# Attention's operands in the mixer's own tiles, and a product split around the first scores

## The chip, the cores and the metric

One core of a Trainium2 chip runs the whole program: TensorE (PE, with its weight loads shown apart as PEld), VectorE (DVE), ScalarE (ACT), GpSimd (POOL) and SyncE (SP), the last of which only issues transfers. The metric is the device time of one execution in microseconds; of several runs the median is taken. There is one input shape (512 tokens, width 1024, two layers), all in float32.

## The reference

Each of the two layers adds three sub-layers to a residual stream: half a SwiGLU block, a mixer, and another half SwiGLU block. The change lies in the mixer, which runs three token mixers on one normalised input:

```python
h = rms_norm(x, mix_norm[l]) @ w_mix_in[l]
(c_x, c_b, c_c, h_q, h_f, h_i, h_g, f_q, f_k, f_v, f_f) = jnp.split(h, split_at, axis=-1)
y = concat[short_conv_mixer(c_x, c_b, c_c, conv_w[l]),           # 256 channels, width 3
           hgrn2_mixer(h_q, h_f, h_i, h_g, lower_bounds[l], ...),  # 4 heads of 64, a gated recurrence
           fox_mixer(f_q, f_k, f_v, f_f, ...)]                   # 8 heads of 64, causal softmax attention
x = x + y @ w_mix_out[l]
# fox_mixer: q, k normalised per head; logit[t, s] = q_t . k_s + c_t - c_s,  c = cumsum(log f);  o = softmax(logit) @ v
```

## The kernel before

**How numbers are carried.** A float32 product is made of three TensorE products: each operand is split into a rounded high part and the rest (`hi`, `lo`), and `mm3` issues hi·hi, hi·lo and lo·hi (lines 376, 382, 383 of the profile). Weights come by SP into a ring of two tiles `st`; ACT writes the high part and DVE the low part into a ring of three tiles `hl` (lines 362 and 363). Accumulators are PSUM banks in four rings: three `mm`, two `sc`, two `pt`, one `po`.

**The order of work.** The program is traced in Python, and a scheduler then orders each engine's instructions at compile time by priority and readiness. `follow(engine, i)` pins an instruction behind the last one that was given so on that engine. Each engine then runs its instructions strictly in that order. A tile of a pool's ring (a "tag") can be written again once its last reader has finished, and a pool that is opened after another was closed lies on the same addresses, so its tiles wait for the last readers of the old tiles there.

**The mixer.** `mix` opens a pool `mp` for the whole mixer. Inside it a pool `hp` ("hg") holds HGRN2: gates and the tiles `q, S, kb, b` (pairs, one per pair of heads; `b` is the running sum of the log gates, `kb` the key's exponent against it, `S` the recurrent state). HGRN2's two pairs of heads run as generators of 13 steps; beside steps 3 to 22 one step each is drawn from `dense`, which makes attention's normalised queries and keys `qk` (two halves of four heads) and the values `V`. These are token-major products: four banks `mm, mm, mm, po` of 128 tokens, the activation stationary on TensorE, the weight moving. For `V` there are 8 steps of 12 products; 20 of dense's 24 steps fit beside HGRN2, so 4 steps of `V` (48 products) are left when HGRN2 is done.

Then `hp` is closed, and a pool `ap_` ("at") is opened on its addresses. `fox_attend` yields step by step, and between its steps `BESIDE` says how many steps of `rest()` are drawn: the rest of `dense`, then the short convolution's products (`conv`), then most of the output projection.

**Attention's operands.** For each head, `fox_prep` transposes queries and keys into a `pt` bank (line 1526), ACT and DVE write the high and the low part (lines 1530 and 1531) to two tiles of the ring `t`, and SP copies them in six transfers of 64 partitions (line 1538) into four stacked operands, `QA, KA` (128 rows) and `QB, KB` (66 rows, with the decay `negc` in the last two; line 1522). Heads alternate between two sets of these tiles. `scores` multiplies them in `sc` banks (line 1565), `turn` transposes the softmax weights (line 1602), `values` multiplies them with `V` (line 1620). The heads' scores come in two parts: part 0 for the first 256 queries, part 1 for the others.

All of `QA, KA, QB, KB`, and the two tiles of ring `t` between, lie in `ap_`, that is, on `hp`'s addresses. HGRN2's last instruction in `hp` is the read of line 1424, which makes the low part `hy` of its output.

## Time and profile before

| | us |
|---|---|
| median of 3 runs | 1849.82 |
| lowest and highest | 1848.95, 1850.83 |
| the profiled execution | 1855.04 |
| its span | 1853.0 |
| mean granted TensorE clock | 0.993 |
| first scores, layer 0 and layer 1 (start of line 1565) | 486.95, 1400.15 |

The profiled execution is 5.2 us (0.28%) longer than the median of the runs, and its span is 2.0 us shorter than its own time. All places below are microseconds from the start of the span. Rows of a timeline give start, duration, engine, line, operation, destination and sources, the shape, and in brackets how long the engine had been idle and what released it. A row of the view by windows gives, for each engine, busy time with the number of instructions, then the granted clock, the share of time that the 16 DMA engines were busy, and GB/s.

### The profile page before, as it was taken

The numbers are of one execution on the slowest core, as the hardware profiler recorded it, in microseconds if no ns is written. First come the engines' busy times: TensorE is split into PE (matmuls) and PEld (weight loads), VectorE is DVE, ScalarE is ACT, GpSimd is POOL, SyncE is SP. The second block draws the span as 40 slices with busy tenths as digits, with TensorE's granted clock in tenths as the row PEclk, the third lists the DMA queues.
The fourth block names the chain that finished last, engine by engine and source line by source line (L and its number), as shares of the span: only waits on it lengthen the run. The fifth ranks groups of instructions, "written<-read, shape, count | busy, mean of one in ns | idle before, by whom it ended". The sixth has DMA issues, their size and how long they took to land.

```text
span 1853.0 us, 32031 instructions
## 1 busy us (share of the span) xinstructions
PE 1831.0 (99%) x12939; PEld 1681.2 (91%) x12939; DVE 1447.7 (78%) x1965; ACT 1004.4 (54%) x1415; POOL 184.7 (10%) x190
## 2 busy tenths in 40 slices
PE   9999999999899999999999999999998999999999
PEld 6899999888788899999989999998887888999997
DVE  7889887679576888878678887966786777987883
ACT  5455554465566555555445555545655664555552
POOL 0011120100000011112001111201000001021210
PEclk9999999999899999999999999999998999999999
DMA  7658784242343667868266787823324429577662
GB/s 204 182 119 191 182 177 96 69 127 69 97 111 101 206 136 180 183 172 171 76 199 139 171 187 186 171 58 89 107 69 112 123 86 238 140 158 199 147 144 91
DMA packets 249908, 262.38 MB, mean 142 GB/s; under 512 B 19816, under 2 KB 228464, under 8 KB 249760
## 3 DMA queue, kind: packets, MB, share of 16 engines
q1 hardware_dynamic: 193344, 191.63, 34.6%
q0 software_dynamic: 55840, 68.19, 23.1%
q8 instruction: 101, 1.65, 0.4%
q10 hardware_dynamic: 576, 0.52, 0.1%
q14 instruction: 47, 0.39, 0.1%
HBM read 226.15 MB, written 2.17 MB: 123 GB/s over the span
## 4 chain that ended last, share of the span: by engine, by line
PE 94%; DVE 3%; ACT 2%; DMA 1%; issue 1%; SPq 0%; DVEq 0%; ACTq 0%
PE mm L376 14%; PE mm L383 13%; PE mm L382 13%; PE sc L376 6%; PE sc L382 6%; PE sc L383 6%; PE pt L376 6%; PE pt L382 6%; PE pt L383 6%; PE po L376 3%; PE po L383 3%; PE po L382 3%; PE sc L1565 2%; PE po L1620 1%; PE sc L1382 1%; PE pt L1602 1%
## 5 line engine op out<-in xcount | busy, mean ns | idle before, releaser
L809 ACT CAST hl<-w 128x1024 fp32r<-128x1024 f32 x322 | 337.6, 1050 | 346.7 <-PE mm L383 81.9
L811 DVE TENSOR_TENSOR hl<-w,hl 128x1024 fp32r<-128x1024 f32 x322 | 393.0, 1222 | 86.1 <-ACT hl L809 85.9
L363 DVE TENSOR_TENSOR hl<-st,hl 128x1024 fp32r<-128x1024 f32 (+3 forms) x152 | 160.2, 1054 | 128.4 <-ACT hl L362 127.9
L362 ACT CAST hl<-st 128x1024 fp32r<-128x1024 f32 (+3 forms) x152 | 138.7, 912 | 176.8 <-PE po L383 83.4
L376 PE MATMUL mm<-xc,hl 128*128 128x256 f32 (+1 forms) x730 | 201.5, 276 | 0.3 <-ACT g L908 0.3
L383 PE MATMUL mm<-xc,hl 128*128 128x256 f32 x728 | 201.4, 277 | 0.0
L382 PE MATMUL mm<-xc,hl 128*128 128x256 f32 x728 | 201.3, 277 | 0.0
L376 PE MATMUL sc<-xc,hl 128*128 128x256 f32 (+1 forms) x530 | 146.4, 277 | 0.6 <-ACT g L908 0.6
L383 PE MATMUL sc<-xc,hl 128*128 128x256 f32 x528 | 146.2, 277 | 0.0
L382 PE MATMUL sc<-xc,hl 128*128 128x256 f32 x528 | 146.1, 277 | 0.0
L376 PEld LDWEIGHTS mm<-xc,hl 128*128 128x128 f32 x730 | 137.0, 188 | 0.8 <-ACT g L908 0.5
L382 PEld LDWEIGHTS mm<-xc,hl 128*128 128x128 f32 x728 | 136.9, 188 | 0.0
L383 PEld LDWEIGHTS mm<-xc,hl 128*128 128x128 f32 x728 | 136.7, 188 | 0.1
L376 PE MATMUL pt<-xc,hl 128*128 128x256 f32 (+1 forms) x482 | 132.7, 276 | 0.0
L382 PE MATMUL pt<-xc,hl 128*128 128x256 f32 x480 | 132.7, 276 | 0.0
L383 PE MATMUL pt<-xc,hl 128*128 128x256 f32 x480 | 132.6, 276 | 0.0
L376 PE MATMUL mm<-x,hl 128*128 128x512 f32 x272 | 111.0, 408 | 0.0
L382 PE MATMUL mm<-x,hl 128*128 128x512 f32 x272 | 107.4, 395 | 0.0
L383 PE MATMUL mm<-x,hl 128*128 128x512 f32 x272 | 107.3, 394 | 0.0
L376 PEld LDWEIGHTS sc<-xc,hl 128*128 128x128 f32 x530 | 99.6, 188 | 1.5 <-ACT g L908 1.0
L383 PEld LDWEIGHTS sc<-xc,hl 128*128 128x128 f32 x528 | 99.1, 188 | 0.1
L382 PEld LDWEIGHTS sc<-xc,hl 128*128 128x128 f32 x528 | 99.2, 188 | 0.0
(478 smaller groups left out, 5489.0 us busy)
## 6 DMA issues: line engine op xcount, KB each, us to landing
w<-in_ffn_w_in_dram SPq DMA_DIRECT2D x140, 512.0 KB
w<-in_ffn_w_out_dram SPq DMA_DIRECT2D x64, 512.0 KB
w<-in_ffn_w_out_dram POOLq DMA_DIRECT2D x56, 512.0 KB, 8.4
st<-in_w_mix_in_dram SPq DMA_DIRECT2D x80, 256.0 KB
w<-in_ffn_w_in_dram POOLq DMA_DIRECT2D x39, 512.0 KB, 8.0
st<-in_ffn_w_in_dram SPq DMA_DIRECT2D x70, 256.0 KB
w<-S POOLq DMA_DIRECT2D x35, 512.0 KB, 4.7
st<-in_ffn_w_out_dram SPq DMA_DIRECT2D x24, 512.0 KB
```

What stands on the lines that cost most here:

```text
L362: a = nc.scalar.copy(hi, src[:, c : c + w])
L363: b = nc.vector.tensor_sub(lo, src[:, c : c + w], hi)
L376: i = nc.tensor.matmul(acc[:, c], ah, bh[:, c], start=first and c.start == 0, stop=False, skip_group_check=True,)
L382: nc.tensor.matmul(acc, ah, bl, start=False, stop=False, skip_group_check=True)
L383: i = nc.tensor.matmul(acc, al, bh, start=False, stop=last, skip_group_check=True)
L809: A(nc.scalar.copy(hi, src))
L811: return lambda: V(nc.vector.tensor_sub(lo, src, hi))
L1382: nc.tensor.matmul(s2[:, :, t], e[:, i * P : (i + 1) * P], e2[:, :, t], start=True, stop=True)
L1565: mm = lambda *a, **k: E(nc.tensor.matmul(*a, skip_group_check=True, **k))
L1602: E(nc.tensor.transpose(tb[:, k * P : (k + 1) * P], to[u][:, j * P : (j + 1) * P], self.ident))
L1620: E(nc.tensor.matmul(self.ob[:, o], half[2][:, j, h].rearrange("p a d -> p (a d)"), part[:, at[0] : at[-1] + 1, :].rearrange("p b t -> p ( ...
```

## The change

```diff
-BESIDE = (2, 2, 1) + (1, 1, 2, 2, 1, 2, 2) + (1, 2, 2, 2, 2, 2, 1, 2, 2)
+BESIDE = (3, 2, 1) + (1, 1, 2, 1, 1, 2, 2) + (1, 2, 2, 2, 2, 2, 1, 2, 2)
...
                 elif not (halves and acc is jobs[-1][0]):
-                    self.mm3(acc, ah[:, toks], al[:, toks], hi[:, cols], lo[:, cols], first, stop)
+                    self.mm3(
+                        acc, ah[:, toks], al[:, toks], hi[:, cols], lo[:, cols], first, stop, False, keep
+                    )
...
-                q, S, kb, b = (pair(hp, tag) for tag in ("q", "S", "kb", "b"))
+                b, kb, q, S = (pair(mp, tag) for tag in ("b", "kb", "q", "S"))
+                negc = mp.tile([NH, 2, T], F32R, tag="n", name=self.n("negc"))
...
             with tc.tile_pool(name=self.n("at"), bufs=1) as ap_:
-                self.tt, self.tb = "t", 4
+                self.tt, self.tb = "t", 2
...
-        tl = lambda p, tag, n=1: pool.tile([p, T], F32R, tag=tag, name=self.n(tag), bufs=n)
-        QA, KA = (tl(P, f"{t}{h % 2}") for t in ("QA", "KA"))
-        QB, KB = (tl(66, f"{t}{h % 2}") for t in ("QB", "KB"))
+        tl = lambda tag: self.mp.tile([P, T], F32R, tag=tag, name=self.n(tag))
+        hi, lo = tl("b0"), tl("b1")
+        if h % 2:
+            QA, KA, QB, KB = (tl(t) for t in ("S0", "S1", "q0", "q1"))
+        else:
+            A = self.mp.tile([P, 2, T], F32R, tag="n", name=self.n("A"))
+            QA, KA, QB, KB = A[:, 0, :], A[:, 1, :], tl("kb0"), tl("kb1")
+        QB, KB = QB[:66, :], KB[:66, :]
...
-        hi, lo = (tl(P, self.tt, self.tb) for _ in range(2))
```

Three things change. First, `q, S, kb, b` and `negc` move from `hp` to `mp`, and attention's operands take over their tiles one by one: the transposed parts `hi, lo` go to HGRN2's `b0, b1`, even heads' operands to `negc`'s tile (now a pair `A`) and `kb0, kb1`, odd heads' to `S0, S1, q0, q1`. Each waits for its own tile's last reader and no longer for the whole of `hp`. The ring `t` of `ap_` shrinks from four tiles to two, and `hi, lo` have one pair of tiles. Second, `keep` is handed on for token-major products, so that `V`'s stand in the given order among the scores. Third, `BESIDE` draws three steps of `V` ahead of the first scores in place of two, and one step less at its seventh place. No product, eviction or transfer is added or removed.

The order of each engine is the same as before up to the end of HGRN2 and again from the later heads on. Three places, in layer 0 (layer 1 has the same rows), show what moves.

TensorE, where the first scores stand: `mm_4730`, `mm_4731` and `po_4732` are banks of `V`, and in the version before `KA, QA, KB, QB` are head 0's operands. Before:

```order
L382 MATMUL po_4732<-hl_5048,x_406_3680 128x512
L383 MATMUL po_4732<-hl_5048,x_406_3680 128x512
L1565 MATMUL sc_5012<-KA_640_4950,QA_639_4949 128x128
L1565 MATMUL sc_5012<-KB_642_4952,QB_641_4951 128x128
L1565 MATMUL sc_5012<-KA_640_4950,QA_639_4949 128x256
L1565 MATMUL sc_5012<-KB_642_4952,QB_641_4951 128x256
L1565 LDWEIGHTS identb
L1565 MATMUL sc_5012<-maskb,identb 128x2x128
L1526 MATMUL pt_5031<-ident,qk_4165 128x128 x4
L1565 MATMUL sc_5078<-KA_640_4950,QA_639_4949 128x384
L1565 MATMUL sc_5078<-KB_642_4952,QB_641_4951 128x384
L1565 LDWEIGHTS identb
```

and now, with `A`, `kb` as head 0's operands (line numbers of the new file):

```order
L382 MATMUL mm_4730<-hl_5010,x_406_3680 128x512
L383 MATMUL mm_4730<-hl_5010,x_406_3680 128x512
L1570 MATMUL sc_5028<-A_4951 128x128
L1570 MATMUL sc_5028<-kb_643_4953,kb_642_4952 128x128
L1570 MATMUL sc_5028<-A_4951 128x256
L1570 MATMUL sc_5028<-kb_643_4953,kb_642_4952 128x256
L1570 LDWEIGHTS identb
L1570 MATMUL sc_5028<-maskb,identb 128x2x128
L1532 MATMUL pt_5049<-ident,qk_4166 128x128 x4
L376 MATMUL mm_4731<-hl_5010,x_404_3673 128x512
L382 MATMUL mm_4731<-hl_5010,x_404_3673 128x512
L383 MATMUL mm_4731<-hl_5010,x_404_3673 128x512
```

The first part of head 0's scores now stands 12 products of `V` earlier (those of `mm_4731` and `po_4732` come after it, and 12 products of the convolution after these), and its second part follows only then.

ScalarE, at the end of HGRN2, before (`t_4893` to `t_4916` are its output norm, `hy` its output, `t_4960` head 0's high part):

```order
L300 ACTIVATE t_4893<-t_4893 128x512
L300 ACTIVATE t_4894<-t_4893 128x512
L300 ACTIVATE t_4915<-sc_4932,epsc 128x512
L300 ACTIVATE t_4915<-t_4915 128x512
L300 ACTIVATE t_4916<-t_4915 128x512
L1423 CAST hy_4929<-t_4891 128x512
L362 CAST hl_5221<-st_5218 128x1024
L1506 ACTIVATE V_4728<-mm_4729,invc_3906 128x8x64
L1506 ACTIVATE V_4728<-mm_4730,invc_3906 128x8x64
L1423 CAST hy_4942<-t_4913 128x512
L1506 ACTIVATE V_4728<-mm_4731,invc_3906 128x8x64
L1530 ACTIVATE t_4960<-pt_4955,qkg_3693 128x512
```

and now (`b_639` is head 0's high part, `b_662` head 1's):

```order
L300 ACTIVATE t_4893<-t_4893 128x512
L1535 ACTIVATE b_639_4949<-pt_4956,qkg_3693 128x512
L300 ACTIVATE t_4894<-t_4893 128x512
L300 ACTIVATE t_4915<-sc_4932,epsc 128x512
L300 ACTIVATE t_4915<-t_4915 128x512
L300 ACTIVATE t_4916<-t_4915 128x512
L362 CAST hl_5181<-st_5178 128x1024
L1425 CAST hy_4929<-t_4891 128x512
L1507 ACTIVATE V_4728<-mm_4729,invc_3907 128x8x64
L1507 ACTIVATE V_4728<-mm_4730,invc_3907 128x8x64
L1425 CAST hy_4942<-t_4913 128x512
L1535 ACTIVATE b_662_5041<-pt_5049,qkg_3693 128x512
```

Head 0's high part moves ahead of ten instructions, into the middle of HGRN2's output norm; VectorE's low part moves likewise, ahead of that norm's first step there. On SP the six copies of head 0 follow, ahead of one more pair of weight transfers that stood before them.

SP, around the copies for the third head (`QA_687, KA_688, KB_690` before; `A_5160, kb_689, kb_690` now), before:

```order
L1522 DMA KB_690_5150<-negc_4365 2x512
L1538 DMA QA_687_5147<-t_5158 64x512
L1538 DMA KA_688_5148<-t_5158 64x512 x2
L1538 DMA QB_689_5149<-t_5158 64x512
L1538 DMA QA_687_5147<-t_5159 64x512
L1538 DMA KB_690_5150<-t_5159 64x512
L1522 DMA KB_718_5275<-negc_4365 2x512
L330 DMA st_5605<-in_w_mix_in_dram 128x4x256
```

and now:

```order
L330 DMA st_5516<-in_w_mix_in_dram 128x4x256
L1528 DMA kb_690_5162<-negc_4365 2x512
L330 DMA st_5602<-in_w_mix_in_dram 128x4x256
L1543 DMA A_5160<-b_686_5158 64x512 x3
L1543 DMA kb_689_5161<-b_686_5158 64x512
L1543 DMA A_5160<-b_687_5159 64x512
L1543 DMA kb_690_5162<-b_687_5159 64x512
```

A weight transfer of the convolution (`st_5605` before, `st_5602` now, 512 KB) goes out ahead of the third head's copies and no longer behind them; on ScalarE and VectorE the split of the granule before it also moves ahead of that head's parts.

More of the change, by code (lines that the diff above doesn't have):

```diff
@@ L1123, in mix @@
                         if step == 8:
-                            self.fox_decay(mp, hp, zf)
+                            self.fox_decay(mp, hp, zf, negc)
             with tc.tile_pool(name=self.n("at"), bufs=1) as ap_:
-                self.tt, self.tb = "t", 4
+                self.tt, self.tb = "t", 2
                 attend = self.fox_attend(ap_, half, qkg)
@@ L1424, in hgrn, with fox_decay @@
         nc.vector.tensor_sub(self.yl[2 + pr], o, self.yh[2 + pr])
-    def fox_decay(self, mp, hp, zf):
+    def fox_decay(self, mp, hp, zf, negc):
         nc = self.nc
@@ L1446, in fox_decay @@
                 )
-        negc = hp.tile([NH, 2, T], F32R, tag="negc", name=self.n("negc"))
         nc.scalar.activation(negc[:, 0, :], cb[:NH, :], AF.Copy, scale=-1.0)
```

## The prediction

> **What bounds the kernel now.** I read the page first (span, busy shares), then TensorE's waits, then the timeline around the longest of them in both layers, then the granted clock by windows. From the page, and from the list of PE's waits (engine, tile and line waiting, what for: us in total, times, longest):

> ```profile
> span 1853.0 us, 32031 instructions
> PE 1831.0 (99%) x12939; PEld 1681.2 (91%) x12939; DVE 1447.7 (78%) x1965; ACT 1004.4 (54%) x1415; POOL 184.7 (10%) x190
> ...
> PE sc L1565 <- DMA QA<-t: 10.7, 2, 5.4
> PE po L519 <- DVE sqa L500: 2.7, 1, 2.7
> ...
> PE sc L1565 <- ACT P L300: 0.9, 2, 0.5
> ```

> TensorE is the bound: only what it waits for, or runs slowly in, can be won. Two waits make up 10.7 us, one per layer: the first scores wait for the copies of head 0's operands. Layer 0's timeline there, then the same places in layer 1:

> ```profile
> 480.49 0.68 DVE L1424 TENSOR_TENSOR hy<-t,hy 128x512 fp32r<-128x512 f32 x1
> 481.20 0.39 PE L383 MATMUL po<-hl,x 128*128 128x512 f32 x1
> 481.25 0.69 ACT L1530 ACTIVATE t<-pt,qkg 128x512 fp32r<-128x512 f32 x1 [0.29 <-DVE hy L1424]
> 481.97 0.47 SPq L1538 DMA_DIRECT2D QA<-t  x1
> 486.95 0.44 PE L1565 MATMUL sc<-KA,QA 128*128 128x128 f32 x1 [5.36 <-DMA QA<-t]
> 487.48 0.44 PE L1565 MATMUL sc<-KB,QB 66*128 66x128 f32 x1
> 495.85 0.49 PE L1602 MATMUL pt<-ident,P 128*128 128x128 f32 x3
> ...
> 1394.43 0.39 PE L383 MATMUL po<-hl,x 128*128 128x512 f32 x1
> 1400.15 0.44 PE L1565 MATMUL sc<-KA,QA 128*128 128x128 f32 x1 [5.33 <-DMA QA<-t]
> 1409.78 0.49 PE L1602 MATMUL pt<-ident,P 128*128 128x128 f32 x3
> ```

> The chain: VectorE's last read in `hp` (line 1424) releases ScalarE's eviction at 481.25, SP's copies follow from 481.97, and TensorE, whose last product of `V` started at 481.20, gets its first operands at 486.95 and the second pair at 487.48. Nothing else is late: the transposes that feed the eviction were done long before (below). The windows (stretch; busy us and count of PE, PEld, DVE, ACT, POOL; granted clock; DMA share; GB/s) show that the wait has a tail:

> ```profile
> 483.00:484.00 1.00, 0.00 (x0) 0.00 (x0) 1.00 (x1) 0.46 (x1) 0.00 (x0) 1.00 0.83 191
> 484.00:484.50 0.50, 0.00 (x0) 0.00 (x0) 0.50 (x2) 0.00 (x0) 0.00 (x0) 0.54 0.90 209
> 486.95:494.46 7.51, 6.96 (x21) 5.17 (x22) 3.31 (x9) 4.12 (x12) 0.52 (x1) 0.51 0.61 154
> 494.50:495.00 0.50, 0.50 (x4) 0.41 (x3) 0.00 (x0) 0.50 (x2) 0.00 (x0) 1.00 0.94 217
> 1398.00:1399.00 1.00, 0.00 (x0) 0.00 (x0) 0.02 (x1) 0.00 (x0) 0.00 (x0) 0.91 0.85 195
> 1400.10:1409.08 8.98, 8.37 (x24) 6.28 (x25) 3.31 (x9) 4.80 (x12) 0.52 (x1) 0.50 0.61 150
> ...
> 36.00:38.00 2.00, 1.21 (x3) 0.72 (x3) 1.80 (x2) 0.71 (x2) 0.00 (x0) 0.72 0.44 155
> 38.00:40.00 2.00, 2.00 (x5) 1.19 (x5) 1.09 (x1) 1.97 (x3) 0.00 (x0) 0.50 0.48 123
> 40.00:42.00 2.00, 2.00 (x10) 1.60 (x9) 1.25 (x3) 1.95 (x3) 0.00 (x0) 0.92 0.59 203
> ```

> While TensorE stood still the granted clock fell to half at about 484.0, and it stayed there for about 7.5 us after work had resumed (in layer 1 from about 1398.8 to 1409, 9 us of it in work). The third idle place, 2.7 us long at line 519, also has half clock after it, for about 3.4 us (from the three windows: 1.12 + 2 + 0.32).

> **What the change can win.** I compare the stretch from the last product of `V` to the first turn with what its work costs at full clock. Rows of the same layer, after the clock is back:

> ```profile
> 496.10 0.31 PE L1565 MATMUL sc<-KA,QA 128*128 128x128 f32 x1
> 496.76 0.60 PE L1526 MATMUL pt<-ident,qk 128*128 128x128 f32 x4
> 497.12 0.48 PE L376 MATMUL mm<-x,hl 128*128 128x512 f32 x1
> 499.94 0.93 PE L1602 MATMUL pt<-ident,P 128*128 128x128 f32 x7
> 500.62 0.42 PE L1565 MATMUL sc<-KA,QA 128*128 128x384 f32 x1
> 501.70 0.36 PE L1620 MATMUL po<-PH,V 128*128 128x256 f32 x1
> ```

> - One product of `V` takes 0.227 us (the last one starts at 481.20; those of the timeline stand 0.227 apart). First-part scores with the next head's transposes: 497.12 − 496.10 = 1.02. Twelve products of the convolution: 499.94 − 497.12 = 2.82. Second-part scores: 501.70 − 500.62 = 1.08. Together 0.227 + 1.02 + 2.82 + 1.08 = 5.15 us.
> - Before, layer 0 took 495.85 − 481.20 = 14.65 and layer 1 took 1409.78 − 1394.43 = 15.35. The excess is 9.50 and 10.20, **19.7 us in all**. The standstill is 5.52 and 5.49 of it (to 486.95 and 1400.15 from 0.227 after the last product), 11.0 in all; the other 8.7 are half clock and the 0.9 us of waits for `P` within it. The windows agree roughly: half of 7.51 and of 8.98 is 8.2.

> Does the change remove the standstill? Where head 0's operands can start from, and when TensorE asks for them:

> ```profile
> 452.09 0.42 DVE L1335 TENSOR_TENSOR t<-b 128x256 f32<-128x256 f32 x1
> 470.00 1.29 ACT L300 ACTIVATE t<-t 128x512 f32<-128x512 f32 x2
> 470.40 0.27 PE L1526 MATMUL pt<-ident,qk 128*128 128x128 f32 x1
> 478.71 0.39 PE L376 MATMUL mm<-hl,x 128*128 128x512 f32 x1
> ```

> Head 0's transposes end at 470.67 already. `b` is last read until 452.5 (first row); the last reads of `kb` and SP's copy of `negc` to DRAM stand ahead of that in the program, so `hi, lo` and head 0's operands find their tiles free. ScalarE and VectorE are inside the output norm then; by the order the eviction goes after the first of ScalarE's two passes, about 470.7, and is done near 471.4. From eviction to the second score product took 481.94 → 487.48, 5.5 us, before; the same again gives operands at **476.9**. TensorE asks 12 products (2.72 us) earlier than 481.43, that is at **478.71**. Slack: 1.8 us. I take no wait there. If the copies collide with weight loads, the first 1.8 us of delay are free, the rest counts one for one.

> The 12 products of `V` that now follow the first scores are moved, not added: cost 0. What their move does is cover: `P`'s softmax chain of head 0 runs under them and under the 12 convolution products.

> **What the change costs.** Per layer:

> - Second-part scores wait for ScalarE's `exp` to free an `sc` bank: 0.46 each before, at half clock. Now the granule's split stands in ScalarE's queue ahead of `exp`, and waits for the last `V` products to release its tile:

> ```profile
> 479.17 1.40 DVE L1507 SCALAR_TENSOR_TENSOR V<-mm,invc,V 128x512 fp32r<-128x512 f32 x2
> 481.84 1.03 ACT L362 CAST hl<-st 128x1024 fp32r<-128x1024 f32 x1
> ```

>   Bounds 0 and 0.5; I take 0.3, nearer the row that exists.
> - `V`'s last evictions on VectorE end at 480.57 before (first row). With head 0's low part (0.75) now ahead, 481.3. The convolution's first product needs the bank at 478.71 + 1.02 + 2.72 = 482.45. Slack 1.1, cost 0; the cover is the 12 products of `V`, and without them each late us would count.
> - Seams of the new interleaving (a `pt` bank, a weight's first load): bounds 0.2 and 0.5, I take 0.4. The norm's squares go round two tiles of the ring `t` instead of four: 0.05.
> - The third head's copies lose their place ahead of a 512 KB load of the convolution's weights:

> ```profile
> 498.74 0.46 SPq L1538 DMA_DIRECT2D QA<-t  x1
> 502.99 0.40 SPq L330 DMA_DIRECT2D st<-in_w_mix_in_dram  x1
> 505.25 0.31 PE L1565 MATMUL sc<-KA,QA 128*128 128x128 f32 x1
> 505.00:506.00 1.00, 1.00 (x10) 0.94 (x9) 0.17 (x1) 1.00 (x4) 0.00 (x0) 1.00 1.06 371
> ```

>   From its transposes (496.76) to its scores (505.25) there are 8.5 us. The copies left at 498.74 and, at head 0's pace (487.48 − 481.97 = 5.5, less about 0.35 for TensorE's own first score) landed by about 503.9: slack 1.35. A load of 512 KB at the 371 GB/s of the last row is 1.4 us, and the split ahead of the parts on ScalarE is another 1.03 (the row of line 362). 2.4 − 1.35 gives 1.1 if both add up, 2.3 if the VectorE half of the split does too, 0 if they overlap with the parts. I take 0.7.
> - HGRN2's output chain on ScalarE and VectorE comes about 0.7 us later each. Its reader is the output projection, beyond the attention heads, so this is free while those stand between. On SP the six copies now stand ahead of one pair of weight transfers that stood before them. That pair is queued behind the copies' wait for the eviction; it last went out just ahead of the copies of 481.97, and the copies are now issued from 471.4 to before 476.9 (they are all landed 5.5 us after the eviction), so the pair goes no later than it did: cost 0.

> Sum per layer: 0.3 + 0.4 + 0.05 + 0.7 = 1.45, bounds 0.2 and 3.3; two layers 2.9. **Net gain 19.7 − 2.9 = 16.8 us.** Durations come from the profiled execution of 1855.04; I take the excess to be the same in the median run, 5.2 us shorter: 1849.8 − 16.8 = **1833.0 us** (1838.2 if the profiled one's surplus comes again).

> **The rivals.**

> - *The wait comes back shorter* (0.12). If head 0's copies or the third head's are more than about 2.5 us late, the clock falls as it did after 2.7 us of idle at line 519. That costs 2.7 + half of 3.4 = 4.4 per layer: 16.8 − 8.8 = 8.0, so 1841.8. For it: the third head's upper bound is 2.3. Against: only 1.1 if just ScalarE and the load add up. Here I also count the case that half clock in this stretch has another cause than the standstill: then only 11.0 − 2.9 = 8.1 is won, 1841.7.
> - *The tail is only partly the standstill's* (0.08). After the third idle place, of 2.7 us, it lasted 3.4 us, not 7.5 to 9 us of work. If a standstill of this kind costs such a tail, 1.7 us each is won and the rest of the slow clock stays: 11.0 + 3.4 − 2.9 = 11.5, so 1838.3. Against: the longer tails stand right behind these very standstills, and no other stretch near them has half clock.
>   [...]
> - *Slower* (0.06). Should the eviction still be released only by HGRN2's end (the pool's release, or its place in ScalarE's queue behind an instruction that itself waits for that end), the operands land at 487.4 as before, while the scores now stand ahead of 12 products of `V` that can no longer cover: TensorE stands 2.72 us longer per layer, 1849.8 + 5.4 = 1855.3. The point that decides: operands later than 478.71 + 5.5 = 484.2 lose, earlier ones win. Against: the one read quoted, of `b`, is over by 452.5, and the eviction stands ahead of the norm's rest in ScalarE's order.
> - *Nothing changes* (0.03): operands near 484.2, standstill as long as before, or a later stage takes all back. That stage would have to idle TensorE for 16 us where the page shows it 99% busy.

> **Chances.** Likeliest case 0.71: both standstills and the half clock go. Its own range from the bounds is 19.7 − 0.4 = 19.3 to 19.7 − 6.6 = 13.1 won, 1830.5 to 1836.7. The range 1829.5 to 1842.0 adds 1 us below for the run-to-run spread shown (1848.95 to 1850.83) and the first rival above; it leaves out about 1 in 10. About 0.2% (3.7 us) can be told from no change here: faster 0.91, same 0.03, slower 0.06.

> **What would show it.** Right: no wait of the first scores for a DMA in PE's list; first scores at about 478.7 in layer 0; granted clock 1.00 through 480 to 496, and in layer 1's stretch; the eviction of head 0 near 470.7; the first turn reached about 5.2 us of work after the last `V`; small waits (under 0.5 us) of second-part scores for `P`; at the third head's scores a wait of about 0.7 for the copies; all stages elsewhere as long as before. Wrong: a wait over 2.4 us at any of these places with 0.5 in the clock after it; the clock at half around 490 without a standstill; or copies that take far longer than 5.5 us while HGRN2's transfers run.

## The result and the profile after

| | us |
|---|---|
| before, median of 4 runs (lowest, highest) | 1849.38 (1848.29, 1850.83) |
| changed, median of 4 runs (lowest, highest) | 1831.41 (1831.13, 1833.18) |
| ratio, 95% interval | 0.9904 (0.9887 to 0.9921) |
| forecast and its range | 1833.0 (1829.5 to 1842.0) |
| profiled execution and span, changed | 1831.55, 1829.8 |

The kernel became 18.0 us faster; 16.8 were forecast. From the page, and from the list of PE's waits (engine, tile and line waiting, what for: us in total, times, longest), changed kernel:

```profile
span 1829.8 us, 32009 instructions
PE 1821.3 (100%) x12939; PEld 1674.5 (92%) x12939; DVE 1446.0 (79%) x1965; ACT 1002.4 (55%) x1415; POOL 185.1 (10%) x190
...
PE po L1709 <- DVE none L215: 1.6, 1, 1.6
...
PE po L521 <- DVE sqa L502: 0.5, 1, 0.5
...
PE sc L1570 <- ACT P L300: 0.4, 2, 0.2
```

The wait of the first scores for a DMA, 10.7 us before, is gone from the list. What is left for the scores is 0.2 us per layer for `P`. The timeline of layer 0, with two rows of layer 1 behind it (line numbers of the new file: 1532 transposes, 1535 the high part, 1536 the low part, 1570 scores, 1607 turn; 478.90 is the last product of `V`, 486.09 the first turn):

```profile
467.01 0.27 PE L1532 MATMUL pt<-ident,qk 128*128 128x128 f32 x1
467.32 0.69 ACT L1535 ACTIVATE b<-pt,qkg 128x512 fp32r<-128x512 f32 x1
468.04 0.75 DVE L1536 SCALAR_TENSOR_TENSOR b<-pt,qkg,b 128x512 fp32r<-128x512 f32 x1 [6.28 <-ACT b L1535]
475.33 0.23 PE L1570 MATMUL sc<-A 128*128 128x128 f32 x1
475.39 0.28 PE L1570 MATMUL sc<-kb,kb 66*128 66x128 f32 x1
478.90 0.39 PE L383 MATMUL po<-hl,x 128*128 128x512 f32 x1
482.62 0.50 PE L1570 MATMUL sc<-A 128*128 128x512 f32 x1 [0.19 <-ACT P L300]
486.09 0.49 PE L1607 MATMUL pt<-ident,P 128*128 128x128 f32 x3
496.00 0.19 PEld L1570 LDWEIGHTS sc<-kb,kb 66*128 66x128 f32 x1 [0.25 <-issue]
533.46 0.49 PE L1607 MATMUL pt<-ident,P 128*128 128x128 f32 x3
...
1369.74 0.27 PE L1532 MATMUL pt<-ident,qk 128*128 128x128 f32 x1
1436.14 0.49 PE L1607 MATMUL pt<-ident,P 128*128 128x128 f32 x3
...
465.00:490.00 25.00, 24.81 (x119) 19.52 (x118) 18.60 (x33) 18.43 (x36) 0.66 (x1) 1.00 0.45 107
1375.00:1400.00 25.00, 24.79 (x134) 20.25 (x133) 17.98 (x35) 18.56 (x38) 1.18 (x2) 1.00 0.53 133
```

The last two rows are windows over the stretch in both layers: TensorE is busy for 24.8 of 25 us at clock 1.00, where it had idled 5.5 us and run at 0.50 after that.

The trace before and the trace after differ by 23.2 us in span, the runs by 18.0. The surplus lies in the profiled execution of before. Head 0's last transpose, ahead of everything that the change moves, starts at 470.40 before and 467.01 after: the wait at line 519 was 2.7 us in the one execution, with 3.4 us of half clock behind it, and the same wait (line 521) was 0.5 us in the other, with none. Another 1.8 us lie between the two mixers (1383.63 − 545.52 = 838.11 against 1369.74 − 533.46 = 836.28); in the traces of the other eight kernels below this stretch takes 836.1 to 838.0 us, with no tie to their passages. I therefore measure each mixer by its **passage**: from that last transpose to one turn near the end of attention, where the order is the same again in all kernels. These rows bound it, before:

```profile
470.40 0.27 PE L1526 MATMUL pt<-ident,qk 128*128 128x128 f32 x1
545.52 0.49 PE L1602 MATMUL pt<-ident,P 128*128 128x128 f32 x3
1383.63 0.27 PE L1526 MATMUL pt<-ident,qk 128*128 128x128 f32 x1
1459.48 0.49 PE L1602 MATMUL pt<-ident,P 128*128 128x128 f32 x3
```

That is 75.12 us in layer 0 and 75.85 in layer 1. After, it is 533.46 − 467.01 = 66.45, and 1436.14 − 1369.74 = 66.40. The saving is 8.67 and 9.45, together 18.1, close to the 18.0 of the runs.

### The profile page after: what moved, and what is told of

Read it like the earlier page. It is cut to its first block, busy times and chain, and to the rows that moved or that the text cites. A ratio compares the mean times of both kernels' runs of the same rounds, so it can differ in the third digit from the quotient of the medians.

```text
span 1829.8 us, 32009 instructions
## 1 busy us (share of the span) xinstructions
PE 1821.3 (100%) x12939; PEld 1674.5 (92%) x12939; DVE 1446.0 (79%) x1965; ACT 1002.4 (55%) x1415; POOL 185.1 (10%) x190
## 3 DMA queue, kind: packets, MB, share of 16 engines
HBM read 226.15 MB, written 2.17 MB: 125 GB/s over the span
## 4 chain that ended last, share of the span: by engine, by line
PE 95%; DVE 2%; ACT 1%; DMA 1%; issue 0%; SPq 0%; DVEq 0%; ACTq 0%
PE mm L376 14%; PE mm L383 14%; PE mm L382 14%; PE sc L376 6%; PE sc L382 6%; PE sc L383 6%; PE pt L382 6%; PE pt L376 6%; PE pt L383 6%; PE po L382 4%; PE po L376 4%; PE po L383 4%; PE sc L1570 1%; PE po L1625 1%; PE sc L1384 1%; PE pt L1607 1%
## 5 line engine op out<-in xcount | busy, mean ns | idle before, releaser
L362 ACT CAST hl<-st 128x1024 fp32r<-128x1024 f32 (+3 forms) x152 | 138.6, 912 | 174.8 <-PE po L383 83.0
L376 PE MATMUL mm<-xc,hl 128*128 128x256 f32 (+1 forms) x730 | 201.6, 277 | 0.3 <-ACT g L910 0.3
L383 PE MATMUL mm<-xc,hl 128*128 128x256 f32 x728 | 201.6, 277 | 0.0
L376 PE MATMUL sc<-xc,hl 128*128 128x256 f32 (+1 forms) x530 | 146.5, 277 | 0.6 <-ACT g L910 0.6
L383 PE MATMUL sc<-xc,hl 128*128 128x256 f32 x528 | 146.3, 277 | 0.0
L376 PEld LDWEIGHTS mm<-xc,hl 128*128 128x128 f32 x730 | 137.1, 188 | 0.8 <-ACT g L910 0.5
L383 PEld LDWEIGHTS mm<-xc,hl 128*128 128x128 f32 x728 | 136.8, 188 | 0.1
L376 PE MATMUL pt<-xc,hl 128*128 128x256 f32 (+1 forms) x482 | 132.8, 276 | 0.0
L383 PE MATMUL pt<-xc,hl 128*128 128x256 f32 x480 | 132.7, 276 | 0.0
L376 PE MATMUL mm<-x,hl 128*128 128x512 f32 x272 | 108.9, 400 | 0.0
L383 PE MATMUL mm<-x,hl 128*128 128x512 f32 x272 | 106.2, 391 | 0.0
L382 PE MATMUL mm<-x,hl 128*128 128x512 f32 x272 | 106.0, 390 | 0.0
L376 PEld LDWEIGHTS sc<-xc,hl 128*128 128x128 f32 x530 | 99.6, 188 | 1.5 <-ACT g L910 1.0
L383 PEld LDWEIGHTS sc<-xc,hl 128*128 128x128 f32 x528 | 99.2, 188 | 0.1
```

Of the source, the lines that this page charges most:

```text
L362: a = nc.scalar.copy(hi, src[:, c : c + w])
L376: i = nc.tensor.matmul(acc[:, c], ah, bh[:, c], start=first and c.start == 0, stop=False, skip_group_check=True,)
L382: nc.tensor.matmul(acc, ah, bl, start=False, stop=False, skip_group_check=True)
L383: i = nc.tensor.matmul(acc, al, bh, start=False, stop=last, skip_group_check=True)
```

## The experiments

Eight more kernels ran, the first four below on one chip and the last four on another. The runs of before beside them have medians of 1851.43 (the first four) and 1852.17 (the last four), so kernels are compared by the ratio, or by the difference to those runs. The passages come from each kernel's trace, in layer 0 and 1. A passage is one execution's, and how much half clock it holds can come out otherwise in another: behind waits of 2.21 us, tiles_only has none in one layer and 3.41 us in the other (last section), and the mean clock of the five runs of tiles_all_v_first goes from 0.997 to 0.999.

| kernel | median | against before | ratio, 95% interval | passages | saved in the two |
|---|---|---|---|---|---|
| full change | 1831.41 | −18.0 | 0.9904 (0.9887 to 0.9921) | 66.45, 66.40 | 18.1 |
| tiles_only | 1838.12 | −13.3 | 0.9930 (0.9917 to 0.9942) | 68.09, 69.67 | 13.2 |
| order_only | 1852.45 | +1.0 | 1.0008 (0.9999 to 1.0016) | 76.26, 75.74 | −1.0 |
| fill22 | 1847.67 | −3.8 | 0.9983 (0.9974 to 0.9992) | 74.08, 74.01 | 2.9 |
| fill12 | 1849.37 | −2.1 | 0.9993 (0.9983 to 1.0003) | 75.14, 75.19 | 0.7 |
| tiles_keep | 1833.58 | −18.6 | 0.9906 (0.9890 to 0.9922) | 67.18, 67.18 | 16.6 |
| tiles_all_v_first | 1839.65 | −12.5 | 0.9936 (0.9923 to 0.9949) | 70.94, 70.13 | 9.9 |
| odd_in_at | 1832.03 | −20.1 | 0.9892 (0.9878 to 0.9905) | 66.03, 66.38 | 18.6 |
| order_fill34 | 1848.39 | −3.8 | 0.9976 (0.9967 to 0.9985) | 74.60, 74.34 | 2.0 |

**The tiles alone (tiles_only).** The change without its new numbers in `BESIDE` and without `keep`; the scheduler then puts the first scores 7 products of `V` earlier than the full change does, and leaves 16 products between the two parts of head 0's scores, where the full change has 24.

```diff
-BESIDE = (3, 2, 1) + (1, 1, 2, 1, 1, 2, 2) + ...
+BESIDE = (2, 2, 1) + (1, 1, 2, 2, 1, 2, 2) + ...
-  self.mm3(acc, ah[:, toks], ..., first, stop, False, keep)
+  self.mm3(acc, ah[:, toks], ..., first, stop)
```

> Only the tile move (b, kb, q, S, negc to the mixer's pool, attention's operands in their places); the old numbers of steps and V's products left to the scheduler, which puts the first scores about 7 products of V earlier than the full change does. Theory (the win is the release of head 0's eviction from the pool's last reader): all of the gain, about 1832, within 3 us of the full change, no wait of over 0.5 us at the first scores and clock 1.00. Rival (the given order and the new numbers carry a good part): over 1836, with a wait at the first scores or the second part.

Its waits, timeline (one row of each layer) and windows:

```profile
PE sc L1568 <- ACT P L300: 4.4, 2, 2.2
...
482.08 0.50 PE L1568 MATMUL sc<-A 128*128 128x512 f32 x1 [2.21 <-ACT P L300]
1388.12 0.50 PE L1568 MATMUL sc<-A 128*128 128x512 f32 x1 [2.21 <-ACT P L300]
...
476.00:492.00 16.00, 13.79 (x76) 11.00 (x75) 11.84 (x24) 12.02 (x26) 0.92 (x2) 1.00 0.62 154
1389.20:1392.61 3.41, 3.41 (x10) 2.64 (x9) 1.09 (x4) 2.01 (x4) 0.29 (x1) 0.50 0.45 148
```

The wait for the copies is gone, so the release is what the tiles do. But the theory's "all of the gain" was wrong: 13 of the 18 us came. `P`'s `exp` is now late by 2.21 us in each layer, and in layer 1 half clock of 3.41 us (the window from 1389.20) came after that wait. The full change has neither this wait nor the half clock, and what it has beyond tiles_only is the order alone; the difference is 4.9 us in the passages.

**The order alone (order_only).** The kernel before with both edits above the other way round: new numbers, given order, old tiles.

> Only the order: new numbers of steps and V's products in the given order, with the operands in the old tiles, released by HGRN2's end. Theory (a wait covered by less work): the first scores are asked for 2.7 us earlier in each layer and the operands land when they did, so the standstill grows from 5.5 to about 8.2 us and the time by 5.4, to about 1855. Rival (the order is what helps): below 1849. A clock that stays at half longer after a longer standstill would make it 1857 to 1859.

```profile
PE sc L1567 <- DMA QA<-t: 16.1, 2, 8.1
...
478.45:488.69 10.24, 4.61 (x15) 3.90 (x16) 2.76 (x7) 2.65 (x7) 0.94 (x2) 0.50 0.40 93
1393.22:1400.05 6.83, 3.60 (x13) 3.09 (x14) 1.04 (x3) 1.51 (x6) 0.00 (x0) 0.50 0.43 98
...
484.01 0.45 PE L1567 MATMUL sc<-KA,QA 128*128 128x128 f32 x1 [8.10 <-DMA QA<-t]
1396.37 0.45 PE L1567 MATMUL sc<-KA,QA 128*128 128x128 f32 x1 [8.05 <-DMA QA<-t]
```

The waits grew by 16.1 − 10.7 = 5.4 us, as expected to the tenth. The time did not: +1.0, with an interval that includes no change. An account from the rows gives 4.8 of the 5.4 back. Half clock lay further inside the standstill: of it 488.69 − 484.01 = 4.68 and 1400.05 − 1396.37 = 3.68 us fell on work, against 7.33 (486.95 to 494.28) and 8.90 (1400.15 to 1409.05) before, and half of the difference is 3.9. (Products of 512 columns start 0.43 us apart at half clock, in the trace of before at 492.47, 492.89 and 493.32, and 0.227 apart at 1.00: nearly half of the time is lost.) The 0.9 us of waits for `P` vanished too, under the 24 products that now stand between the parts.

**The standstill filled (fill22, fill12).** In the kernel before, useless products occupy TensorE while it waits. `V`'s products are pinned ahead of them, where they stood anyway.

```diff
-BESIDE = (2, 2, 1) + ...
+BESIDE = (4, 0, 1) + ...          # with keep handed on in mm3, as in the change
     b = self.bank("sc")           # in scores(h, 0)
+    for _ in range(22 if h == 0 else 0):
+        E(nc.tensor.matmul(b, self.xact(0)[0][:, :P], self.xact(0)[0], start=True, stop=True))
```

> The kernel before, with 22 products (128x512, 0.227 us each, 5.0 us) of a live operand into the scores' own bank ahead of the first scores of each layer; the scores overwrite them, so the output is the same. They fill the standstill of 5.5 us but don't shorten it. Theory (half clock is caused by the standstill): clock 1.00 throughout, the standstill of 11.0 us in two layers stays, the 8.7 us of half clock go: about 1841. Rival (half clock there has another cause, such as the transfers or the small products after it): 1849, clock 0.5 as before.

```profile
478.00:495.00 17.00, 14.51 (x72) 11.31 (x71) 8.64 (x18) 8.99 (x22) 1.51 (x3) 1.00 0.58 142
...
484.22 0.30 PE L1569 MATMUL sc<-KA,QA 128*128 128x128 f32 x1 [0.39 <-DMA QA<-t]
487.42 0.50 PE L1569 MATMUL sc<-KA,QA 128*128 128x512 f32 x1 [1.07 <-ACT P L300]
490.87 0.49 PE L1606 MATMUL pt<-ident,P 128*128 128x128 f32 x3
491.81 0.30 PE L1569 MATMUL sc<-KA,QA 128*128 128x128 f32 x1 [0.45 <-DMA QA<-t]
492.44 0.30 PE L1569 MATMUL sc<-KB,QB 66*128 66x128 f32 x1 [0.34 <-DMA KB<-negc]
```

The clock is at 1.00 throughout, in layer 1 too (1390 to 1410), so the standstill caused the half clock; the rival falls. (Of the 11 runs 8 have a mean clock of 1.000, and the three slowest 0.998; before it was 0.992 to 0.994.) But of 8.7 us only 3.8 came (2.9 in the passages). The rows say why: at full clock TensorE ran into the next late things. `exp` now costs 1.07 us (0.46 before), and head 1's scores wait, 0.45 and 0.34, for the copies of their operands, where before they followed the turn without a wait. From the first scores to the first turn fill22 is 2.2 us ahead in layer 0 (490.87 − 484.22 = 6.65 against 495.85 − 486.95 = 8.90); of that 1.0 is left in the passage. TensorE at half speed had hidden that the chains of heads 0 and 1 were both late.

> As with 22 products, but 12 (2.7 us), which leaves TensorE idle for about 2.8 us of the 5.5. If 2.4 us of idle time is enough for half clock, as in the trace of before, the clock falls again: with a tail of 3.4 us, as after the 2.7 us at line 519, about 1844; with the long tail of 10 us, about 1849. [...]

```profile
482.22 0.30 PE L1569 MATMUL sc<-KA,QA 128*128 128x128 f32 x1 [2.68 <-DMA QA<-t]
...
483.47:490.30 6.83, 6.37 (x19) 4.58 (x18) 3.31 (x9) 4.74 (x12) 0.52 (x1) 0.50 0.68 175
1394.83:1401.66 6.83, 6.37 (x20) 4.58 (x18) 3.31 (x9) 4.75 (x12) 0.52 (x1) 0.50 0.67 174
```

After an idle time of 2.7 us the clock does fall to 0.50 here, for 6.83 us in both layers: neither the 3.4 nor the 10 that I had offered. The time is that of before within the interval.

**`keep` with the old numbers (tiles_keep).** The full change with `BESIDE` as before, so that the first scores stand another 12 products earlier.

> The tile move and V's products in the given order, with the old numbers of steps: the first scores stand 12 products (2.7 us) earlier than in the full change, with 24 products of V between them and the second part. In the full change the last copies of head 0 are issued 1.6 to 2.2 us per layer after the eviction begins to be copied and land about 2 us ahead of the scores. Theory (what counts is when the operand chain can end, and enough products behind the first scores): a wait of 0.5 to 1 us at the first scores, no half clock, within 2 us of the full change, 18 us under the kernel before. Rival (the wait trips the clock again): half clock of 3.4 us or more, 1835 to 1840.

```profile
472.87 0.30 PE L1570 MATMUL sc<-A 128*128 128x128 f32 x1 [0.35 <-DMA A<-b]
473.94 0.30 PE L1570 MATMUL sc<-kb,kb 66*128 66x128 f32 x1 [0.77 <-DMA kb<-b]
1377.60 0.30 PE L1570 MATMUL sc<-kb,kb 66*128 66x128 f32 x1 [0.35 <-DMA kb<-b]
```

As the theory had it: waits of 0.35 and 0.77 us, clock at 1.00, 1.5 us less saved than by the full change in the passages, and not to be told from it in the runs. It also measures when the operands can be used: the second pair at 473.94 in layer 0, 7.16 us after that trace's last transpose (466.78), and at 1377.60 in layer 1, 6.58 us after (1371.02).

**All of `V` ahead of the first scores (tiles_all_v_first).** The full change with `BESIDE = (4, 0, 1) + (1, 1, 2, 2, 1, 2, 2) + ...`: the second part of head 0's scores follows the first at once, as in the kernel before.

> The full change, but all of V ahead of the first scores (numbers 4, 0, 1 in place of 3, 2, 1, and two again at the seventh place), so that the second-part scores follow the first at once, as in the kernel before. Theory (beside the release of head 0, head 1's chain needs cover: exp frees the sc bank, and head 1's copies take 5.5 us from its transposes): waits for exp of about 1.1 us and for head 1's copies of about 0.7 us per layer, 3 to 4 us slower than the full change, so 14 to 15 us under the kernel before. Rival (only head 0's release counts): within 1 us of the full change.

```profile
PE sc L1570 <- ACT P L300: 4.3, 2, 2.2
...
481.16:487.99 6.83, 6.43 (x16) 4.64 (x17) 2.75 (x8) 3.03 (x8) 0.52 (x1) 0.50 0.78 193
1389.11:1392.52 3.41, 3.41 (x9) 2.41 (x10) 2.43 (x6) 1.99 (x6) 0.52 (x1) 0.50 1.00 282
```

8.2 us worse than the full change by the medians and by the passages, 5.5 by each kernel's difference to its own runs of before: more than expected either way, and far from the rival. The wait for `exp` is 2.17 us per layer (0.19 in the full change), and half clock of 6.83 and 3.41 us comes with it: 2 × 2.0 for the waits and at most 5.1 for the clock. This execution had more half clock than the kernel's other runs (mean clock 0.997 against 0.998 and 0.999). So with the tiles moved, a third to nearly a half of the gain still depends on what stands between the two parts of head 0's scores.

**Odd heads' operands as before (odd_in_at).** Only `b, kb, negc` move.

```diff
-b, kb, q, S = (pair(mp, tag) for tag in ("b", "kb", "q", "S"))
+b, kb = (pair(mp, tag) for tag in ("b", "kb"))
+q, S = (pair(hp, tag) for tag in ("q", "S"))
...
-    QA, KA, QB, KB = (tl(t) for t in ("S0", "S1", "q0", "q1"))
+    QA, KA, QB, KB = (pool.tile([P, T], F32R, tag=t, ...) for t in ("QA1", "KA1", "QB1", "KB1"))
```

> The full change, but only b, kb and negc leave HGRN2's pool; q and S stay in it, and odd heads' operands lie in attention's pool, released by HGRN2's end as before. Everything else is in the same order on TensorE, ScalarE and VectorE. Theory (only head 0's chain has to start before HGRN2's end; head 1's parts exist only after it anyway): the same as the full change within 1 us. Rival (head 1's copies wait for the pool and come late): a wait for head 1's operands of 1 us or more per layer, 2 us or more slower.

The same as the full change: 18.6 us saved in the passages against 18.1, and the intervals of the ratios overlap, so no better version is claimed. Moving `q` and `S` has no share in the gain that these runs can tell.

**The order alone with the standstill filled (order_fill34).** As fill22, with 34 products, in order_only's order.

> The kernel with the new order and the old tiles, with 34 filling products (7.7 us) in the standstill of 8.1 us ahead of each layer's first scores, so that the clock should stay at 1.00. The order alone had half clock for 10.2 and 6.8 us. Theory (in this stretch the operand chains of heads 0 and 1, not TensorE, set the pace, and the half clock lies in their shadow): 0 to 3 us faster than the order alone. Rival (half clock costs half of its length wherever TensorE has products to do): (10.2 + 6.8) / 2 = 8.5 us faster than the order alone.

```profile
475.00:495.00 20.00, 19.38 (x93) 15.53 (x92) 9.84 (x18) 8.90 (x20) 1.51 (x3) 1.00 0.54 132
1390.00:1410.00 20.00, 19.40 (x97) 15.66 (x96) 9.20 (x18) 9.88 (x21) 1.51 (x3) 1.00 0.48 116
```

The clock stays at 1.00, and the kernel is 4.1 us faster than order_only by the medians (1848.39 against 1852.45), 4.8 by the differences to each one's runs of before, and 3.1 in the passages: far from the rival, and above the theory's 3 us, though in the passages only just. The rival's 8.5 had counted the half clock that lay in the standstill, where it is free. On work lay 4.68 + 3.68 = 8.4 us, and half of that is 4.2. Here 24 products cover `exp` and head 1's copies, and half clock costs about half of the work that it covers, as near as the three numbers can tell. A shadow of the full size is thus seen only without that cover, as in fill22, where half of 7.33 + 8.90 would be 8.1 and 3.8 were measured.

## Why the prediction was right, and which terms were not

- **The mechanism.** The eviction was expected near 470.7 and runs at 467.32, which is 470.71 with the 3.39 us by which this execution is ahead. The first scores were expected at 478.71; 475.33 + 3.39 = 478.72. No wait for a DMA, clock 1.00: as forecast.
- **The slack of the operands** was put at 1.8 us. tiles_keep shows the second pair 7.16 us after the last transpose in layer 0 and 6.58 in layer 1; the full change asks for it 475.39 − 467.01 = 8.38 after: slack 1.2 and 1.8. In layer 0 the copies take 0.7 us longer than the 5.5 that I took over. It cost nothing, but the cover was thinner there.
- **The first turn** was expected about 5.2 us of work after the last product of `V`, and it came 486.09 − 478.90 = 7.19 after. That sign was put wrongly: it took over the work of the old order, and in the new one 24 products of the convolution stand in this place and no longer 12. The passages are not touched by this.
- **The excess** of 19.7 us was recovered almost whole. Costs were put at 1.45 per layer; 9.50 − 8.67 = 0.83 and 10.20 − 9.45 = 0.75 were measured. The second-part scores wait 0.19 (0.3 taken). At the third head a weight load starts 0.25 late in layer 0, the row at 496.00 (0.7 taken), and the trace names no copy as its cause; in odd_in_at the wait at this place in layer 1 is 0.15 us and named as one for a copy. So if the copies are late there, it is by a few tenths. The 0.4 for seams and the 0.05 for the ring had no row behind them and were not measured by themselves; in layer 0, 0.83 − 0.19 − 0.25 leaves about 0.4 us for them.
- **The split into 11.0 of standstill and 8.7 of half clock** was the weak step. The sum is right, yet the second term is not there to be had by itself: 3.8 us by fill22. The rest of it stood for late `exp` and late copies of head 1, which the full change removes by other means, by starting the chain 10 us earlier and by the 24 products between the parts. That the whole 8.7 came nevertheless is in part luck: the sum had not asked what else was late. I had written "cost 0, what their move does is cover" for those products; without that cover 5.5 to 8.2 us of the gain are lost (tiles_all_v_first).
- **The rival with slower as its end** was priced at +5.4; order_only, its mechanism made real, gave +1.0. The wait itself grew by 5.4. What failed is the sum "one us of wait, one us of time" beside a resource, the clock, whose loss moved with the wait: of half clock 16.2 us fell on work before and 8.4 in order_only.
- **The rival of the shorter tail** gave the half clock 1.7 us per layer, 3.4 in all, close to the 3.8 of fill22, though for another reason: the tail is no shorter, it hides late operands. Its time of 1838.3 did not come, because the full change takes that lateness away too.

Not settled: how much of what the cover is worth each of the two, `exp` and head 1's copies, carries by itself. `keep` was not run alone; with the new numbers every engine has the same instructions in the same order with and without it, so in the full change it adds nothing, and the order there is the work of `BESIDE`. With the old numbers it does tell: tiles_keep saved 3.4 us more in the passages than tiles_only.

## What to carry to other kernels

A stall, the slow clock behind it and the lateness of the next operands overlapped here: by the sum half clock was worth 8.7 us, and 3.8 came by fill22. What each costs has to be asked by taking away one of them, not by adding up the trace. Look for the cause at the head of the chain (here one pool's release, a tile's last reader in place of the pool's) and then give the next link of the chain products to hide under; here the first alone brought 13 us (tiles_only), the second alone nothing that the runs can tell (order_only), both together 18.

## What the hardware showed that I had not expected

```profile
480.00:484.00 4.00, 1.59 (x8) 0.97 (x6) 3.68 (x5) 3.00 (x5) 0.98 (x2) 1.00 0.63 171
484.04:494.28 10.24, 6.79 (x21) 5.06 (x22) 4.06 (x11) 3.94 (x11) 0.52 (x1) 0.50 0.68 166
494.28:500.00 5.72, 5.72 (x33) 4.79 (x32) 2.39 (x7) 2.85 (x8) 0.00 (x0) 1.00 0.18 42
...
1398.81:1409.05 10.24, 8.34 (x24) 6.28 (x25) 3.31 (x9) 4.80 (x12) 0.52 (x1) 0.50 0.65 157
36.90:40.31 3.41, 3.41 (x7) 1.98 (x8) 2.12 (x2) 2.41 (x4) 0.00 (x0) 0.50 0.39 111
```

In four traces the starts lie whole units apart. A third of 10.24 is 3.4133; before, (484.04 − 36.90) / 3.4133 = 131.0 and (1398.81 − 484.04) / 3.4133 = 268.0, and between the two starts (windows above) it is 268.0 units in order_only, 267.0 in fill12 and 266.0 in tiles_all_v_first.

The same wait came with a fall and without one. In tiles_only TensorE waited 2.21 us in both layers. In layer 1, from 1385.91 to 1388.12, the wait lies whole in the unit that ends at 1389.20, and there the clock fell; in layer 0, from 479.87 to 482.08, the clock stayed at 1.00. An estimate from the spacing above, 266 units back from 1389.20, puts an end of a unit at 481.25, which would cut layer 0's wait into 1.38 and 0.83. Of the unit ahead of a fall TensorE was idle for 2.66, 2.45 and 3.41 us before (ahead of 36.90, 484.04 and 1398.81), and for 1.77 in layer 0 of tiles_all_v_first (the wait began at 479.39, the clock fell at 481.16). In fill22, which waits 1.8 us at line 521, a stretch as long as a unit held 1.75 us of idle time, and the clock stayed at 1.00 in it and behind it:

```profile
34.80:38.21 3.41, 1.66 (x6) 1.08 (x7) 2.54 (x3) 2.20 (x4) 0.00 (x0) 1.00 0.46 150
38.21:41.62 3.41, 3.41 (x17) 2.81 (x16) 2.30 (x3) 3.33 (x5) 0.00 (x0) 1.00 0.63 181
```

Where such units begin in that trace is not shown, and the ends of products in a profile are modelled, so no limit can be read from 1.75 and 1.77. In the windows shown here the clock came back after a unit in which TensorE was idle for at most 0.07 us: before, the three units from 484.04 hold 2.97, 0.49 and 0.00 us of idle time, those from 1398.81 hold 1.44, 0.46 and 0.00, the one from 36.90 holds 0.00, and the clock is at 1.00 behind the last of each. The wait of 0.46 us for `P` lies in the second unit of each layer there. Half clock of a single unit has 0.00 us of idle time in tiles_only (from 1389.20) and in tiles_all_v_first (from 1389.11); half clock of two units has 0.40 in tiles_all_v_first (from 481.16) and 0.46 in fill12 (from 483.47), each a wait in the first of the two; the second unit of layer 1 in order_only has the 0.07 (1396.82 to 1396.89). Why it should be so, no run here shows.
